# Attention values: transposed probabilities split into high and low halves, one key-value head at a time

## The chip, the cores and the metric

One NeuronCore of a Trainium2 chip runs the whole program. The metric is the device time of one execution in microseconds (us); the kernel before has a median of 1749.84 us over 3 runs (1747.56 to 1750.02).

## The reference

Two layers of a hybrid bidirectional backbone over 512 latent tokens and 256 context tokens, all in fp32. Layer 0 mixes with gated linear attention (GLA) beside grouped-query attention, layer 1 with mLSTM beside retention; every layer has an MLP. Only the attention of layer 0 is touched:

```python
def softmax_attend(q, k, v):
    s = jnp.einsum('bkgqd,bksd->bkgqs', q, k).astype(jnp.float32) * (q.shape[-1] ** -0.5)
    p = jax.nn.softmax(s, axis=-1).astype(v.dtype)
    return jnp.einsum('bkgqs,bksd->bkgqd', p, v)
...
    k_all = jnp.concatenate([k_c, k_l], axis=2)
    v_all = jnp.concatenate([v_c, v_l], axis=2)
    att_l = merge(blocked_attend(group_q(q_l), k_all, v_all).reshape(q_l.shape))
...
    att_c = merge(softmax_attend(group_q(q_c), k_c, v_c).reshape(q_c.shape))
```

There are 8 query heads of 64 in groups of g = 4 on 2 key-value heads (kv). Latent queries see all 768 keys, context queries the 256 context keys.

## The kernel before

The 768 tokens are 6 tiles t of 128; t = 0, 1 are context and see nk = 2 key tiles kt, t = 2 to 5 see nk = 6, so there are 28 pairs (t, kt). Products that want fp32 accuracy are mostly made of F32R operands: a tensor is split into a high half (a cast to F32R on ACT, L197) and a low half (a subtraction on DVE, L198), and `mm3` (L488, L489, L490) multiplies high by high, high by low and low by high, three matmuls into one accumulator. The attention is one function (L1051) with two generators:

- `scores_kv` (step S): for each t, kv and g, matmuls of 512 and 256 columns (L1093) into a PSUM tile of tag A (2 buffers), the row's maximum on DVE (L1095), and exp with its row sum on ACT (L1096) into P.
- `values` (step V), one step per key tile: for kv 0 and kv 1, four PE transposes of P (L1107) into a PSUM tile of tag B (2 buffers), copied to SBUF (tag PT, 4 buffers) by ACT for kv 0 (L1110) and by DVE for kv 1 (L1112). After the yield come two plain fp32 matmuls (L1116) of 64 stationary columns, kv 0 into the upper and kv 1 into the lower 64 partitions of one PSUM tile `po` (tag O, 1 buffer). After the last kt: reciprocal of the row sums (L1118), its transpose (L1120), copy (L1122), four matmuls with `sel` that spread it over the partitions (L1125), copy to R (L1127), and the product `po` times R on DVE (L1129). Then `finish` splits the tile into high and low (L1144, by L197 and L198): it is half of the input of the output projection.

The string PLAN["att"] writes out the order: S, V, Q (a query tile from DRAM), f (`fill`: one tile of a projection with its `mm3` matmuls, or nothing once those are used up), M (`gating`: one of four products of the GLA output, transposed at L1244 and split). The program's scheduler may still exchange neighbouring instructions when it builds, after which each engine runs its own list in order.

Three things tie the end of the attention to what follows. `sel` lies in a buffer of the tag wh, in which the high halves of weights lie too. The weights of the output projection are loaded per k = 0 to 7 (`w_out_unit`, DMAs at L540 and L541 on SP's queue for k of 4 and more) into raw buffers (tag raw, 3 of them) and split by L197 and L198; the high half of k = 4 takes the buffer of `sel`, and the raw buffer that k = 4 frees is the one into which k = 7 is loaded. And the projection's first matmuls (its k below 4 don't need the attention) stand on PE's list among and behind the last steps of the attention.

The values v (and the keys, `ak`) come out of a projection at the start, evacuated by `ev0`: one ACT copy per token tile for v (L1182).

## Time and profile before

| | |
|---|---|
| median of 3 runs | 1749.84 us (1747.56 to 1750.02) |
| profiled execution | 1746.07 us, of which the span on the core is 1744.4 us |
| mean granted TensorE clock | 0.981 |
| PE busy | 1660.3 us (95% of the span), 9795 matmuls |
| DVE busy | 1131.3 us (65%) |
| ACT busy | 791.5 us (45%) |
| POOL busy | 264.3 us (15%) |
| chain that ended last, by engine | PE 77%, DVE 9%, DMA 6%, ACT 4%, issue 3% |
| the attention's steps | from about 275 to 436 us of the span |

PE is the engine to look at over the whole program, but a share of a span is a mean over stages. The attention is a tenth of the span, and it has stretches with `fill` matmuls from other work on PE and stretches without; so the views below are taken by stretch: 275 to 367 us (steps f among the others), 367 to 417 us (none left), and 417 us on (the last query tile's values and the start of the output projection). The chain of waits lists, in order of time, what each piece of the way to the end waited for; the windows give busy time per engine in a stretch.

### The profile page before, as it was taken

The page shows a single profiled execution, that of the slowest core. Times are in us where ns is not written, and L with a number is a line of the kernel's source. Part 1 is how long each engine was busy: PE and PEld are TensorE (multiplying, and loading weights), DVE is VectorE, ACT ScalarE, POOL GpSimd, SP SyncE. Part 2 cuts the span into 40 slices and gives each one's busy share as a digit, 9 for nine tenths or more (in the row PEclk, how much of TensorE's full clock was granted, in tenths as well). Part 3 has the DMA queues.
Part 4 walks back from the last instruction along what each step waited for, and adds up shares of the span by engine and source line. Part 5 has one row for each costly group of instructions (what it writes and reads, how often), then busy time and mean ns, then how long its engine had stood idle before and what let it go on. Part 6 is the DMA issues. An engine that isn't in the chain of part 4 may idle for free.

```text
span 1744.4 us, 25127 instructions
## 1 busy us (share of the span) xinstructions
PE 1660.3 (95%) x9795; PEld 1316.5 (75%) x9795; DVE 1131.3 (65%) x1678; ACT 791.5 (45%) x1392; POOL 264.3 (15%) x216
## 2 busy tenths in 40 slices
PE   7998999999999999999999999978998999999998
PEld 5775555755778888888888878757887788888876
DVE  5435456465678558657668693466786676777876
ACT  5335435464345434334333454635552355445443
POOL 0000020100002211121120000164011112223210
PEclk9999999999999999999999999988996999999999
DMA  9415666231654224224123552234545533333322
GB/s 289 129 52 178 202 205 223 72 91 37 205 169 128 90 61 155 74 83 157 62 90 118 176 192 64 84 104 130 161 132 164 181 98 108 110 108 99 107 86 84
DMA packets 174746, 220.67 MB, mean 127 GB/s; under 512 B 17450, under 2 KB 112742, under 8 KB 174628
## 3 DMA queue, kind: packets, MB, share of 16 engines
q1 hardware_dynamic: 169444, 201.24, 36.7%
q0 software_dynamic: 5184, 17.83, 3.0%
q8 instruction: 77, 1.26, 0.3%
q14 instruction: 41, 0.34, 0.1%
HBM read 193.74 MB, written 25.30 MB: 126 GB/s over the span
## 4 chain that ended last, share of the span: by engine, by line
PE 77%; DVE 9%; DMA 6%; ACT 4%; issue 3%; SPq 1%; POOL 0%; DVEq 0%; ACTq 0%; POOLq 0%
PE x L488 21%; PE x L489 21%; PE x L490 21%; DMA x<-in_ada_w_dram 2%; PE x L1116 2%; PE x L260 2%; DVE x L198 2%; PE x L1107 1%; PE x L1093 1%; DMA x<-x 1%; ACT x L197 1%; PE x L1542 1%; PE x L957 1%; PE x L435 1%; PE x L1681 1%
## 5 line engine op out<-in xcount | busy, mean ns | idle before, releaser
L488 PE MATMUL x<-x,x 128*128 128x512 f32 (+2 forms) x2042 | 763.3, 375 | 12.1 <-ACT x L197 3.4
L489 PE MATMUL x<-x,x 128*128 128x512 f32 (+2 forms) x2050 | 762.8, 373 | 7.1 <-DVE x L198 7.1
L490 PE MATMUL x<-x,x 128*128 128x512 f32 (+2 forms) x2050 | 761.1, 372 | 0.1
L198 DVE TENSOR_TENSOR x<-x,x 128x1024 fp32r<-128x1024 f32 (+4 forms) x373 | 395.5, 1079 | 216.5 <-ACT x L197 211.4
L197 ACT CAST x<-x 128x1024 fp32r<-128x1024 f32 (+4 forms) x373 | 332.7, 911 | 388.4 <-PE x L489 181.3
L488 PEld LDWEIGHTS x<-x,x 128*128 128x128 f32 x2042 | 387.4, 190 | 91.1 <-ACT x L197 9.0
L489 PEld LDWEIGHTS x<-x,x 128*128 128x128 f32 x2050 | 389.1, 190 | 75.7 <-DVE x L198 11.7
L490 PEld LDWEIGHTS x<-x,x 128*128 128x128 f32 x2050 | 388.9, 190 | 70.6 <-issue 6.3
L638 POOL TENSOR_TENSOR x<-x,x 128x1024 f32<-128x1024 f32 x56 | 145.5, 2599 | 546.3 <-DMA x<-in_mlp_w_dram 250.2
L744 DVE TENSOR_TENSOR x<-x,x 128x512 f32<-128x512 f32 x225 | 143.9, 680 | 12.3 <-PE x L490 11.2
L689 ACT ACTIVATE x<-x 128x512 f32<-128x512 f32 (+4 forms) x96 | 44.3, 477 | 91.2 <-PE x L490 91.2
L312 DVE SCALAR_TENSOR_TENSOR x<-x,x,x 128x512 f32<-128x512 f32 x56 | 53.1, 948 | 20.8 <-DMA x<-in_ada_w_dram 19.9
L260 PE MATMUL x<-x,x 128*32 128x512 f32 x192 | 45.6, 604 | 7.5 <-DMA x<-in_ada_w_dram 7.4
L690 ACT ACTIVATE x<-x 128x512 f32<-128x512 f32 (+4 forms) x96 | 48.0, 516 | 2.1
L1095 DVE TENSOR_REDUCE x<-x 128x1 f32<-128x768 f32 (+1 forms) x48 | 36.6, 775 | 18.9 <-PE x L1093 18.7
L1116 PE MATMUL x<-x,x 128*64 128x512 f32 x112 | 44.2, 618 | 1.0 <-ACT x L1110 0.7
L1096 ACT ACTIVATE x<-x,x 128x768 f32<-128x768 f32 (+1 forms) x48 | 36.3, 757 | 12.5 <-DVE x L1095 12.3
L1107 PEld LDWEIGHTS x<-x,x 128*128 128x128 f32 x224 | 24.5, 141 | 22.9 <-issue 21.1
L675 DVE TENSOR_TENSOR x<-x 128x768 f32<-128x768 f32 (+1 forms) x28 | 38.4, 1371 | 0.0
L1093 PE MATMUL x<-x,x 128*128 128x256 f32 (+1 forms) x160 | 36.7, 347 | 1.3 <-ACT x L1096 1.3
L799 DVE TENSOR_REDUCE x<-x 128x8 f32<-128x512 f32 (+1 forms) x19 | 14.3, 753 | 35.5 <-ACT x L797 35.4
L797 ACT ACTIVATE x<-x 128x512 f32<-128x512 f32 (+1 forms) x19 | 12.8, 673 | 47.6 <-PE x L957 25.8
(316 smaller groups left out, 1517.8 us busy)
## 6 DMA issues: line engine op xcount, KB each, us to landing
x<-in_mlp_w_dram SPq DMA_DIRECT2D x128, 512.0 KB
x<-in_ada_w_dram SPq DMA_DIRECT2D x96, 512.0 KB
x<-x SPq DMA_DIRECT2D x42, 512.0 KB
x<-x SPq DMA_DIRECT2D x50, 256.0 KB
x<-in_cd_w_in_dram SPq DMA_DIRECT2D x24, 512.0 KB
x<-x POOLq DMA_DIRECT2D x36, 256.0 KB, 3.1
x<-in_ab_w_in_dram SPq DMA_DIRECT2D x16, 512.0 KB
x<-x SPq DMA_DIRECT2D x20, 384.0 KB
```

What stands on the lines that cost most here:

```text
L197: self.nc.scalar.copy(hi, src)
L198: self.nc.vector.tensor_tensor(out=lo, in0=src, in1=hi.bitcast(F32), op=ALU.subtract)
L260: nc.tensor.matmul(ps[32 * g:32 * g + 32, :n], self.sT[:, k, :], rs[g], start=k == 0, stop=k == 7)
L312: nc.vector.scalar_tensor_tensor(out=acc[x], in0=w, scalar=c, in1=acc[x], op0=ALU.mult, op1=ALU.add)
L488: mm(out, st[0], mv[0], start=start, stop=False, skip_group_check=partial)
L489: mm(out, st[0], mv[1], start=False, stop=False, skip_group_check=partial)
L490: mm(out, st[1], mv[0], start=False, stop=stop, skip_group_check=partial)
L638: sub = lambda out, x, y: nc.gpsimd.tensor_tensor(out=out, in0=x, in1=y, op=ALU.subtract)
L690: nc.scalar.activation(out=hh[:, f, c0:c1], in_=h[:, c0:c1], func=AF.Square)
L744: nc.vector.tensor_tensor(out=dst, in0=dst, in1=acc[j], op=ALU.add)
L1093: mm(pS[:, s0:s1], qs[:, h * 128:(h + 1) * 128], kst[kv][i][:, s0:s1], start=i == 0, stop=i == 1)
L1116: mm(po[64 * kv:64 * kv + 64, :], av[:, kt * 128 + kv * 64:kt * 128 + kv * 64 + 64], PT[kv], start=kt == 0, stop=kt == nk - 1)
```

## The change

- `values` takes kv in its outer loop and kt in its inner one. One step is one pair (kv, kt): four transposes (L1106), the split of their PSUM tile into high (ACT, L197) and low (DVE, L198), and after the yield two F32R matmuls (L1111), of the high and of the low half, with 128 stationary columns: v high and v low side by side.
- v is split as it is projected (`ev0`): per token tile two casts and two subtractions of 128x64 take the place of one copy; for kv 1 the halves change sides.
- `po` then holds the product with v high in one half of its partitions and that with v low in the other. After the last kt of a kv, ACT copies one half to SBUF (`sums`, L1114) and DVE adds the other (L1115). `po` has one buffer as before, so it must be emptied before the next kv's first L1111.
- The product with R is made on GpSimd (L1128), from `sums`. `sums` is the other half of the buffer that holds `sel`.
- PLAN["att"] has two V for each one before, 62 steps in place of 34.
- `ak` moves into a buffer that was already there, and `lr` shares one with X; this makes room for the larger `av`.

```diff
-            po = self.po()
-            for kt in range(nk):
-                PT = []
-                for kv in range(2):
+            for kv in range(2):
+                po = self.po()
+                for kt in range(nk):
                     pt = self.pb()
                     for g in range(4):
                         nc.tensor.transpose(pt[:, g * 128:(g + 1) * 128], P[kv][:, g, kt * 128:(kt + 1) * 128], self.C["ident"])
-                    o = self.T(at, [128, 512], F32, tag="PT", bufs=4)
-                    if kv == 0:
-                        nc.scalar.copy(o, pt)
-                    else:
-                        nc.vector.tensor_copy(o, pt)
-                    PT.append(o)
-                yield
-                for kv in range(2):
-                    mm(po[64 * kv:64 * kv + 64, :], av[:, kt * 128 + kv * 64:kt * 128 + kv * 64 + 64], PT[kv], start=kt == 0, stop=kt == nk - 1)
+                    hi, lo = [self.T(at, [128, 512], F32R, tag="PT", bufs=4) for _ in range(2)]
+                    self.split(hi, lo, pt)
+                    yield
+                    for x in (hi, lo):
+                        mm(po, av[:, kt, kv], x, start=kt == 0 and x is hi, stop=kt == nk - 1 and x is lo)
+
+                r, q = (slice(64 * x, 64 * x + 64) for x in (kv, 1 - kv))
+                nc.scalar.copy(sums[r], po[q])
+                nc.vector.tensor_tensor(out=sums[r], in0=sums[r], in1=po[r], op=ALU.add)
...
-            nc.vector.tensor_tensor(out=o, in0=po, in1=R, op=ALU.mult)
+            nc.gpsimd.tensor_tensor(out=o, in0=sums, in1=R, op=ALU.mult)
...
-        sel = self.T(self.w1, [128, 1024], F32R, tag="wh").bitcast(F32)[:8, :512]
+        sel = self.T(self.w1, [128, 1024], F32R, tag="wh").bitcast(F32)
+        sel, sums = sel[:8, :512], sel[:, 512:]
...
-                    nc.scalar.copy(av[:, t * 128:(t + 1) * 128], ps[:, 128:256])
+                    for kv in range(2):
+                        v = ps[:, 128 + kv * 64:192 + kv * 64]
+                        hi, lo = (av[:, t, kv, x * 64:x * 64 + 64] for x in (kv, 1 - kv))
+                        self.split(hi, lo, v)
...
-    "att": "QQSSSSQSSSfSVSfSSSVSfSSSVfQSSSVSSVSSSVfQfVSSVVSfVSVQSSVSSVfVSVSSVSVSSVSVSVMSVSMVVSSVSSSVVSVMVVVVVVVM",
+    "att": "QQSSSSQSSSfSVVSfSSSVVSfSSSVfQSSSVVSSVVSSSVfQfVVSSVVVVSfVVSVVQSSVVSSVfVVSVVSSVVSVVSSVVSVVSVMSVVSMVVVVSSVVSSSVVVVSVMVVVVVVVVVVVVVM",
```

How this moves instructions shows best at three places. The first is PE's list in the middle stretch, where no step f is left: scores (L1093), transposes and value matmuls alternate. x_3501 is `po` before, x_3593 is `po` now, and the tile at the head of an L1116 or L1111's sources is a transposed tile in SBUF. Before:

```order
L1116 MATMUL x_3501<-x_3564,x_655 64x512
L1116 MATMUL x_3501<-x_3571,x_655 64x512
L1107 MATMUL x_3583<-x_73,x_3270 128x128 x4
L1107 MATMUL x_3590<-x_73,x_3402 128x128 x4
L1093 MATMUL x_3598<-x_1073,x_3220 128x512
L1093 MATMUL x_3598<-x_1073,x_3220 128x256
L1093 MATMUL x_3598<-x_1073,x_3220 128x512
L1093 MATMUL x_3598<-x_1073,x_3220 128x256
L1116 MATMUL x_3501<-x_3588,x_655 64x512
```

Now:

```order
L1111 MATMUL x_3593<-x_3599,x_654 128x512
L1111 MATMUL x_3593<-x_3600,x_654 128x512
L1106 MATMUL x_3625<-x_73,x_3327 128x128 x4
L1111 MATMUL x_3593<-x_3610,x_654 128x512
L1093 MATMUL x_3653<-x_1091,x_3271 128x512
L1093 MATMUL x_3653<-x_1091,x_3271 128x256
L1093 MATMUL x_3653<-x_1091,x_3271 128x512
L1111 MATMUL x_3593<-x_3611,x_654 128x512
L1111 MATMUL x_3593<-x_3630,x_654 128x512
```

The pair of matmuls of one key tile, which stood behind eight transposes, has become two pairs, each of a high and a low half from one set of four transposes, and all for one kv; the second of a pair (from x_3611) stands behind another three score matmuls.

The second place is PE's list at the end of the attention. L488 to L490 are `mm3` matmuls of the output projection, x_4088 before and x_4303 now its first accumulators; L1120 and L1119 are the transpose of the reciprocals, L1125 and L1124 the matmuls with `sel`. Before:

```order
L1107 MATMUL x_3977<-x_73,x_3692 128x128 x4
L1107 MATMUL x_3984<-x_73,x_3801 128x128 x4
L488 MATMUL x_4088<-x_4031,x_3181 128x512
L1116 MATMUL x_3896<-x_3982,x_655 64x512
L1116 MATMUL x_3896<-x_3989,x_655 64x512
L1120 MATMUL x_3994<-x_73,x_2704 8x128
L489 MATMUL x_4088<-x_4032,x_3181 128x512
L490 MATMUL x_4088<-x_4031,x_3182 128x512
L1125 MATMUL x_3998<-x_3996,x_2696 128x128 x4
L488 MATMUL x_4088<-x_4037,x_3181 128x512
L489 MATMUL x_4088<-x_4038,x_3181 128x512
L490 MATMUL x_4088<-x_4037,x_3182 128x512
```

Now:

```order
L1111 MATMUL x_4139<-x_4179,x_654 128x512
L1106 MATMUL x_4195<-x_73,x_3961 128x128
L1111 MATMUL x_4139<-x_4189,x_654 128x512
L1106 MATMUL x_4195<-x_73,x_3961 128x128 x3
L490 MATMUL x_4360<-x_4258,x_3233 128x512
L1111 MATMUL x_4139<-x_4190,x_654 128x512
L1119 MATMUL x_4209<-x_73,x_2721 8x128
L1111 MATMUL x_4139<-x_4200,x_654 128x512
L1124 MATMUL x_4213<-x_4211,x_2713 128x128 x3
L1111 MATMUL x_4139<-x_4201,x_654 128x512
L1124 MATMUL x_4213<-x_4211,x_2713 128x128
L488 MATMUL x_4303<-x_4265,x_3230 128x512
```

Before, 4 `mm3` matmuls stood among the last query tile's key tiles, and 36 between its last L1116 and the first that needs k = 7; now 24 and 18. The transpose of the reciprocals and most matmuls with `sel` now stand ahead of the last L1111.

The third place is ACT's list there; x_4050 before and x_4265 now is the high half of the weights of k = 4, x_4084 and x_4299 that of k = 7, and the cast of 128x4x128 is `finish`. Before:

```order
L1122 COPY x_3996<-x_3994 8x128
L1127 COPY x_4003<-x_3998 128x512
L197 CAST x_4050<-x_4047 128x1024
L197 CAST x_3179<-x_4003 128x4x128
L197 CAST x_4070<-x_4067 128x1024
L197 CAST x_4077<-x_4074 128x1024
L197 CAST x_4084<-x_4081 128x1024
```

Now:

```order
L1121 COPY x_4211<-x_4209 8x128
L1114 COPY x_2713<-x_4139 64x512
L1126 COPY x_4218<-x_4213 128x512
L197 CAST x_3230<-x_4218 128x4x128
L197 CAST x_4265<-x_4262 128x1024
L197 CAST x_4285<-x_4282 128x1024
L197 CAST x_4292<-x_4289 128x1024
L197 CAST x_4299<-x_4296 128x1024
```

The copy out of `po` (L1114) has come in, and `finish`, whose source is now what GpSimd's product leaves, stands ahead of the cast of k = 4 in place of behind it. On SP's list a broadcast (L341) now stands ahead of the load of k = 7, and behind it before; behind the attention every list is the same in both.

## Rows read from the trace of the kernel before

**Rows 1.** Windows by stretch: length in us, then busy us (instructions) of PE, PEld, DVE, ACT, POOL.

```profile
275.00:340.00 65.00, 63.07 (x316) 44.40 (x314) 40.32 (x75) 37.36 (x90) 6.36 (x8) 1.00 0.39 135
340.00:367.30 27.30, 27.27 (x129) 17.87 (x128) 13.42 (x20) 15.80 (x29) 3.16 (x3) 1.00 0.12 42
367.30:417.30 50.00, 49.59 (x255) 28.76 (x253) 35.82 (x46) 29.61 (x59) 1.26 (x1) 1.00 0.32 94
417.30:436.30 19.00, 18.48 (x89) 9.74 (x89) 6.43 (x9) 5.66 (x11) 0.00 (x0) 1.00 0.00 1
```

**Rows 2.** Groups of instructions from 272 to 440 us, shapes kept apart.

```profile
L1116 PE MATMUL x<-x,x 128*64 128x512 f32 x112 | 44.2, 618 | 1.0 <-ACT x L1110 0.7
L1107 PE MATMUL x<-x,x 128*128 128x128 f32 x224 | 32.8, 280 | 0.0
L1095 DVE TENSOR_REDUCE x<-x 128x1 f32<-128x768 f32 x32 | 30.2, 953 | 5.8 <-PE x L1093 5.7
L1096 ACT ACTIVATE x<-x,x 128x768 f32<-128x768 f32 x32 | 28.8, 899 | 7.7 <-DVE x L1095 7.7
...
L1112 DVE COPY x<-x 128x512 f32<-128x512 f32 x28 | 19.3, 689 | 19.3 <-PE x L1107 19.0
L1110 ACT COPY x<-x 128x512 f32<-128x512 f32 x28 | 16.3, 583 | 26.7 <-PE x L1107 26.7
...
L1218 POOL TENSOR_TENSOR x<-x,x 128x512 f32<-128x512 f32 x6 | 7.7, 1283 | 59.4 <-DVE x L222 34.7 <-issue 24.7
```

**Rows 3.** Chain of waits in the middle stretch: start us, us, what.

```profile
367.49 0.23 PE x L490
367.71 0.87 PE x L1107 x8
...
369.29 1.00 PE x L1116 x2
...
383.53 1.02 PE x L1107 x8
...
402.72 1.01 PE x L1116 x4
...
416.55 0.59 PE x L1107 x4
```

**Rows 4.** The same chain near the first value matmuls.

```profile
290.20 0.48 ACT x L1110
...
290.72 1.07 PE x L1116 x2
```

**Rows 5.** The same chain at the end of the attention.

```profile
422.97 0.32 issue
...
432.31 1.56 PE x L1116 x4
...
436.19 1.06 ACT x L197
...
437.28 1.24 DVE x L198
...
438.53 0.47 SPq L540
...
439.05 4.35 DMA x<-in_w_out_dram
...
443.47 1.05 ACT x L197
```

**Rows 6.** TensorE's timeline, the first matmuls that need the weights of k = 7.

```profile
444.57 0.73 PE L488 MATMUL x<-x,x 128*128 128x512 f32 x2 [0.35 <-ACT x L197]
```

**Rows 7.** One line's instructions, L1182: duration ns min/median/max, first and last start us.

```profile
L1182 ACT COPY x<-x x6: 266/272/275, 73.0 to 93.0; 128x128 f32<-128x128 f32 x6
```

**Rows 8.** The page's busy tenths in 40 slices.

```profile
DVE  5435456465678558657668693466786676777876
ACT  5335435464345434334333454635552355445443
```

More of the change, by code (lines that the diff above doesn't have):

```diff
@@ L837, in gla @@
         nc.scalar.copy(lrT, pt[:, :768])
-        X, XC = self.T(ga, [128, 708]), self.T(ga, [128, 256])
+        X, XC = self.T(ga, [128, 708], tag="X", bufs=1), self.T(ga, [128, 256])
         nc.gpsimd.memset(X, 0.0)
@@ L999, in att_tables, with att_keys @@
         return gb, tabs
-    def att_keys(self, ak, gb, tab):
+    def att_keys(self, scr, gb, tab):
         nc = self.nc
         kst = self.big(self.r2, F32R)
-        scr = self.T(self.r2, [128, 3072], F32, tag="big", bufs=4)
-        kt1 = scr[:, 0:768]
+        kt1, ak = scr[:, 0:768], scr[:, 2304:]
         akv = ak.rearrange("p (x c) -> p x c", c=64)
@@ L1164, in layer0 @@
         with self.pool("mx") as mx:
-            ak, av = self.T(mx, [128, 768]), self.T(mx, [128, 768])
+            av = self.T(mx, [128, NT, 2, 128], F32R)
             gb, tabs = self.att_tables(mx)
             gqk = self.big(self.r2)
+            scr = self.T(self.r2, [128, 3072], F32, tag="big", bufs=4)
+            ak = scr[:, 2304:]
             def ev1(t, ps):
@@ L1177, in layer0 @@
                 self.C0 = self.load_consts(ga, _L0_CONST)
-                lr = self.T(ga, [128, 6, 32])
+                lr = self.T(ga, [128, 708], tag="X", bufs=1)[:, :192].rearrange("p (t n) -> p t n", t=6)
                 def ev0(t, ps):
                     nc.scalar.copy(ak[:, t * 128:(t + 1) * 128], ps[:, 0:128])
-                    nc.scalar.copy(av[:, t * 128:(t + 1) * 128], ps[:, 128:256])
+                    for kv in range(2):
+                        v = ps[:, 128 + kv * 64:192 + kv * 64]
+                        hi, lo = (av[:, t, kv, x * 64:x * 64 + 64] for x in (kv, 1 - kv))
+                        self.split(hi, lo, v)
                     nc.vector.tensor_copy(lr[:, t], ps[:, 256:288])
@@ L1188, in layer0 @@
                               lambda t, ps: nc.scalar.copy(tok4(gv, t), ps.rearrange("p (r n) -> p r n", r=4)), True)
-                kst = self.att_keys(ak, gb, tabs[1])
+                kst = self.att_keys(scr, gb, tabs[1])
                 late = []
```

## The prediction, before the change was run

> **What bounds the kernel now.** I read the windows first, since the change touches a tenth of the program. In all four stretches PE is busy nearly throughout: 63.1 of 65.0 us, 27.3 of 27.3, 49.6 of 50.0, 18.5 of 19.0, at a granted clock of 1.00 [rows 1]. DVE has 35.8 and ACT 29.6 of the 50.0 us in the middle stretch [rows 1]: loaded, but not the bound. So time comes from PE first, and the question is how much of it DVE and ACT let through.
>
> Then the groups by shape: the value matmuls L1116 hold PE for 44.2 us, the transposes L1107 for 32.8 [rows 2]. The chain shows what they cost: two records of one fp32 matmul alone take 1.00 us; the four records of a pair of heads, when both are ready, take 1.01, because the two use different columns of the array; when the second copy is late they take up to 1.56 [rows 3, 5]. A pair always overlapped would give 28 x 1.01 = 28.3 us, the row has 44.2, so most pairs run mostly one after the other. An F32R matmul of 512 columns takes 0.23 us in the chain [rows 3]. After fp32 or scores there is a small entry cost: eight transposes take 0.87 us behind F32R work and 1.02 behind L1116 [rows 3].
>
> Last the chain at the end. The last L1116 piece begins at 432.31 and lasts 1.56 us; after it the chain leaves PE: the cast and subtraction of the weights k = 4 (they wait for the buffer of `sel`), SP's issue, a transfer of 4.35 us, the cast of k = 7 [rows 5], whose first matmul is at 444.57 [rows 6]. From 433.87 to that is 10.7 us, in which PE has 36 `mm3` matmuls (8.3 us at 0.23) and L1125 (some 1.1) to run. So this end is tied by two things at once: PE's work, and the chain through the weights.
>
> **The change, part by part.**
>
> *Value matmuls.* 56 fp32 matmuls (112 records, 44.2 us) become 112 in F32R: 112 x 0.23 = 25.8. Freed: 18.4. There are 56 short groups of transposes instead of 28 pairs; 28 more entries at 0 to 0.15 us (1.02 - 0.87) are 0 to 4.2 us. I take 1.4, nearer the lower end, since they stand between F32R work now. **PE work freed: 17.0 us.** By stretch, at 0.61 per pair (17.0 / 28): some 5.6 to 275-367 us, 7.3 to the middle, 3.6 to the last tile.
>
> *Evacuation.* Before, ACT copies kv 0 (583 ns) and DVE kv 1 (689 ns), side by side [rows 2]. Now each of the 56 transposed tiles goes through ACT and then DVE. That is 28 more passes on ACT (16.3 us) and 28 more on DVE (19.3 us), plus 12 ACT copies (at most 7.0) and 12 adds (at most 8.3) out of `po`, less six products on DVE (4.1). And the path from transposes to matmul grows by a DVE pass: about 0.6 + 0.7 and some 0.4 of handovers (0.32 from PE to ACT, 0.03 from ACT to DVE [rows 5]) instead of 0.6 or 0.7, with only two PSUM buffers and four PT tiles to run ahead.
>
> *Middle stretch* (367.71 to 416.55 in the chain, 48.8 us [rows 3], 12 pairs, no filler). PE's own work falls to some 41.5. DVE: 35.8 + 12 more passes and 4 adds less 2 products (14 x 0.69 = 9.7) is 45.5. ACT: 29.6 + 16 passes (9.4) is 39. I followed the three lists against each other with these durations: 46.3 us. So **-2.5**; bounds -6 (PE's work and two entry waits alone) and +2 (DVE's 45.5 with some 5 us of waits at either end).
>
> *First stretches* (92 us, 10 pairs). PE frees 5.6, but the first value matmuls already wait for an ACT copy that stands behind other work (chain: ACT to 290.68, then L1116 at 290.72 [rows 4]); there a DVE pass and its queue come on top, 1 to 2 us twice. **-2.0**; bounds -5.6 and +1.5.
>
> *Last tile* (416.55 to 433.87, 17.3 us). Here 20 more `mm3` matmuls (4.6 us) now stand among the key tiles, so PE's work is: transposes 48 x 0.11 and entries 5.9, L1111 24 x 0.23 = 5.5, `mm3` 5.5, six more transposes 0.7, in all 17.6. The waits for cast and subtraction that the fillers don't cover add some 2.6: 20.2. **+2.9**; bounds 0 and +4.
>
> *End.* The buffer of `sel` now comes free only after `po` is emptied, `sums` added and GpSimd's product made; and `finish`, which waits for that product, stands ahead of the cast of k = 4 on ACT and holds it and the three casts behind it. From the last L1111: copy 0.6, add 0.7, product 1.28 (as L1218 [rows 2]), `finish` 0.6, then cast 1.06, subtraction 1.24, issue 0.47, transfer 4.35, cast 1.05 [rows 5], and some 0.6 for handovers (0.32 to ACT, 0.03 to 0.07 for the others [rows 5]): 11.9 against 10.7. **+1.2**; bounds +0.5 and +2.7 (the broadcast now ahead of this load on SP's queue costs up to three issues of 0.47). PE has only 18 `mm3` matmuls and a rest of L1124 for these 11.9 us, some 4.4, so it idles for 7: that is where the freed time comes out.
>
> *v split.* Twelve casts and twelve subtractions of 128x64 for six copies of 0.27 us [rows 7]: at 0.27 each, a longest side of DVE + 3.2 us. At 73 to 93 us DVE and ACT are 3 to 5 tenths busy (slices 2 and 3 [rows 8]) and PE's projection runs on other accumulators: 0, bounds 0 and +0.5. The single `po` makes a kv's first L1111 wait for copy and add (1.3 us) twelve times; four transposes and scores stand ahead of it on PE each time, so this is inside the walks above.
>
> **Sum:** -2.5 - 2.0 + 2.9 + 1.2 = -0.4 us, so 1745.7 for the profiled execution of 1746.07. That one stands 3.8 below the median of 1749.84; against the median it is 1749.4.
>
> The Trainium skill, "TensorEngine Tiling (Array Packing)", section "Theoretical Speedup", speaks against giving up the narrow tiles: a matrix side of 64 or less lets two tiles run in parallel, for an estimate of 2 times. By that rule alone the old pairs would cost 28.3 us and the change would free 2.5 instead of 18.4; the 44.2 us of the row says that the rule is met in few pairs here, and the measurement decides.
>
> **Rivals.**
>
> *A. PE stays the bound and the evacuation keeps up.* Then the middle gives -6, the first stretches -5.6, the last tile +1 (17.6 and entry gaps), the end +1.2: -9.4, **1740**. For it: PE at 97 to 100% in every stretch [rows 1], DVE with 14 us idle in the middle one. Against: DVE's 45.5 there lies above PE's 41.5.
>
> *B. Slower: the evacuation becomes the bound.* The place is DVE's list in the middle stretch: every L198 waits for its L197, and the maxima of the scores (953 ns, 32 of them [rows 2]) stand in the same list, so each wait delays the next scores and with them exp and the next transposes. It decides once DVE's sum with its waits passes the 48.8 us of today: 45.5 and 24 waits of 0.25 (below the 0.32 between a transpose and its ACT copy [rows 5]) are 51.5, +2.7. The first stretches then give +1.5, the last tile and the end as above: +8.3, **1758**. For it: two engines in series with two PSUM buffers leave little to run ahead. Against: before their copies DVE and ACT now sit idle for 19.0 and 26.7 us, waiting for the transposes [rows 2], and that is room.
>
> The Trainium skill, the same page, section "PSUM Bottleneck", warns of this case: faster tiles do nothing for the emptying of PSUM, which may become the bottleneck, and both ScalarE and VectorE should share it. Here both already do, but in series after the change; no row of before shows that.
>
> *C. The change doesn't do what it says:* the F32R form with 128 stationary columns takes as long as fp32. 112 x 1.00 would add 68 us. The L490 piece of 0.23 is the same type and width, so next to nothing.
>
> **How the numbers follow.** About 0.2% (3.5 us) is what a measurement of this kernel can tell from no change. My forecast, no change that can be told, gets 0.38; A 0.34, B 0.27, C 0.01. The forecast's own range is 1746 to 1753. With cases of both signs holding most of the chance, the range of 8 in 10 takes in A's 1740 and B's 1758, and a microsecond beyond each for the unknown entries and for SP's order: 1739 to 1759. The two outermost sums of all bounds, -11 and +11, lie at its edges. Faster 0.35 (A and a little of the forecast's edge), same 0.38, slower 0.27.
>
> **What would show it.** L1111 112 times at 0.23 us apart. In the middle stretch DVE above nine tenths with waits of L198 on L197, and a length near 46 us; near 42 is A, above 50 is B. The last tile near 20 us. PE idle for some 7 us between the last L1111 and the k = 7 matmuls, with the chain L1114, add, GpSimd's product of 1.28, `finish`, k = 4, DMA. I am wrong if the projection's start does not wait for GpSimd, if L1111 pairs stand further apart than transposes explain, or if stretches outside 275 to 446 us change by over 2 us.

## The result, and the profile after

The changed kernel takes 1760.56 us (median of 4 runs, 1758.71 to 1762.69) where the kernel before took 1748.70 (4 runs, 1745.82 to 1750.02): a ratio of 1.007 with a 95% interval of 1.0051 to 1.009. It is 12 us slower. The forecast was 1749.4 and no change that can be told; the range ended at 1759.

The profiled execution took 1759.3 us, its span 1757.5. To see where the time went I cut both traces at the same landmarks: the first score matmul, the last fill matmul, the first transpose of the last query tile, the end of the last value matmul, the first matmul that needs the weights of k = 7, and one `mm3` matmul behind it (the 276th L490). The windows between them, before the change (columns as in [rows 1]; behind POOL stand the granted clock, the DMA engines' busy share and the GB/s that they moved):

```profile
274.98:367.10 92.12, 90.17 (x443) 62.10 (x442) 53.54 (x94) 52.96 (x119) 9.54 (x11) 1.00 0.31 108
367.10:416.48 49.38, 48.97 (x249) 28.29 (x247) 35.66 (x46) 29.16 (x57) 1.26 (x1) 1.00 0.33 96
416.48:433.86 17.38, 16.86 (x83) 8.53 (x82) 6.79 (x10) 5.47 (x9) 0.00 (x0) 1.00 0.00 1
433.86:444.57 10.71, 10.36 (x48) 7.72 (x48) 4.99 (x7) 5.36 (x7) 1.12 (x2) 1.00 0.41 130
444.57:460.02 15.45, 14.92 (x65) 12.04 (x66) 6.45 (x12) 4.77 (x12) 0.25 (x1) 1.00 0.76 250
```

and after:

```profile
277.76:370.31 92.55, 87.95 (x442) 68.17 (x442) 62.44 (x106) 60.59 (x134) 12.60 (x14) 0.98 0.31 106
370.31:419.42 49.11, 43.14 (x247) 32.80 (x245) 43.72 (x58) 37.03 (x73) 3.33 (x3) 1.00 0.33 94
419.42:440.48 21.06, 20.57 (x113) 15.34 (x111) 11.65 (x17) 10.37 (x19) 1.29 (x1) 1.00 0.00 1
440.48:459.25 18.77, 7.14 (x21) 4.81 (x20) 4.98 (x7) 5.67 (x7) 2.38 (x3) 0.74 0.67 171
459.25:475.95 16.70, 16.66 (x65) 13.16 (x66) 6.45 (x12) 4.76 (x12) 0.25 (x1) 0.88 0.42 122
```

| stretch | before | after | change | forecast |
|---|---|---|---|---|
| first score matmul to last fill | 92.1 | 92.6 | +0.4 | -2.0 |
| middle | 49.4 | 49.1 | -0.3 | -2.5 |
| last tile | 17.4 | 21.1 | +3.7 | +2.9 |
| end: last value matmul to k = 7 | 10.7 | 18.8 | +8.1 | +1.2 |
| behind it, to the same `mm3` | 15.4 | 16.7 | +1.3 | 0 |
| sum | 185.0 | 198.2 | +13.2 | -0.4 |

Where the first score matmul falls is no reading of the change: it lies between 273.5 and 283.8 us in the 14 profiles of these experiments, of kernels with either attention, and at 277.8 in this one against 275.0 before. So the lengths of stretches are compared here, not their starts. (The time ahead of the first landmark is 2.8 us longer in this profile than before, the time behind the last one 2.8 us shorter; within that spread neither can be put down to the change.)

Two things are to be seen. In the first two stretches PE was freed, by 2.2 and 5.8 busy us, and they are as long as they were: PE's idle time grew from 2.0 to 4.6 us and from 0.4 to 6.0. And at the end PE has 7.1 busy us of 18.8. What PE waited for from the first score matmul to the last value matmul is led by one row in both kernels (us in total, times, longest us), before and after:

```profile
PE x L1093 <- ACT x L1096: 1.3, 2, 1.1
```

```profile
PE x L1093 <- ACT x L1096: 4.4, 8, 0.8
```

These are scores that wait for the exp on ACT, which leaves their PSUM tile free. After the change 2.6 us of waits of the value matmuls for cast and subtraction come with it (0.7 for their copies before), and 1.9 of `fill`'s matmuls for ACT's casts (none of 0.2 us or more before). The groups of the changed kernel that answer to [rows 2], from 272 to 446 us:

```profile
L1111 PE MATMUL x<-x,x 128*128 128x512 f32 x112 | 44.1, 442 | 3.1 <-DVE x L198 1.3 <-ACT x L197 1.3
L198 DVE TENSOR_TENSOR x<-x,x 128x512 fp32r<-128x512 f32 x62 | 41.8, 686 | 14.2 <-ACT x L197 13.5
L197 ACT CAST x<-x 128x512 fp32r<-128x512 f32 x62 | 35.7, 588 | 22.3 <-PE x L1106 17.4 <-POOL x L1128 2.9 <-PE x L1111 1.4
L1106 PE MATMUL x<-x,x 128*128 128x128 f32 x224 | 33.3, 272 | 0.0
...
L1128 POOL TENSOR_TENSOR x<-x,x 128x512 f32<-128x512 f32 x6 | 7.8, 1296 | 86.8 <-DVE x L1115 61.0 <-ACT x L1126 25.8
```

L198 and L197 have 62 of these shapes, 56 of them for transposed tiles; DVE stood 13.5 us waiting for ACT's casts ahead of L198, where its copies waited 19.0 us for the transposes before [rows 2]. The busy time of L1111 (44.1 us, as much as L1116 had) is no price of a matmul: a matmul's bar is 442 ns long here, and in the chain below two that stand together take 0.46 us (428.49), as forecast. But one that stands among transposes takes 0.37 (434.42). Counted from each start to the next instruction's start on PE, less idle time, the 31 that stand right behind another L1111 take 0.24 on the mean, those right behind a transpose 0.35, and all 112 together 32.7 us (0.29 each). The 112 records of L1116 took 41.7 by the same count, and the transposes as long as before. So 9.0 us were freed, not the 17.0 of the forecast.

The chain at the end, in order of time (start us, us, what), answers to [rows 5]:

```profile
428.49 0.46 PE x L1111 x2
...
434.42 0.37 PE x L1111
...
440.06 0.44 PE x L1111
...
440.52 0.59 ACT x L1114
...
441.13 0.70 DVE x L1115
...
442.02 1.24 POOL x L1128
...
443.81 1.05 ACT x L197
...
444.88 1.24 DVE x L198
...
446.13 0.47 SPq L540
...
446.65 11.43 DMA x<-in_w_out_dram
...
458.16 1.05 ACT x L197
...
459.25 0.79 PE x L488
```

and SP's queue at the same time:

```profile
444.70 0.33 SPq L341 DMA_DIRECT2D x<-x  x1
446.13 0.47 SPq L540 DMA_DIRECT2D x<-in_w_out_dram  x1
446.65 0.67 SPq L541 DMA_DIRECT2D x<-in_w_out_dram  x1
```

Before, SP issued the load at 438.53 [rows 5] and the broadcasts behind it:

```profile
440.07 1.29 SPq L341 DMA_DIRECT2D x<-x  x3
```

The links from the last L1111 to SP's issue at 446.13 take 5.7 us, as the forecast had them (5.5 and the handovers). The transfer takes 11.43 us where it took 4.35 [rows 5]. In SP's queue the broadcast L341 was issued 1.4 us ahead of it. A second order turned round as well: GpSimd issues two loads of inputs of 512 KB each (L576), before 1.2 us behind the load's issue, and now 0.9 us ahead of it. Before and after:

```profile
439.78 1.12 POOL L576 DMA_DIRECT2D x<-in_ctx_dram  x2 [63.06 <-DVE x L1297]
```

```profile
445.21 1.12 POOL L576 DMA_DIRECT2D x<-in_ctx_dram  x2 [1.96 <-DVE x L1302]
```

### The profile page after: what moved, and what is told of

Its sections match the earlier page's. It is cut to its first block, busy times and chain, and to the rows that moved or that the text cites. A ratio compares the mean times of both kernels' runs of the same rounds, so it can differ in the third digit from the quotient of the medians.

```text
span 1757.5 us, 25288 instructions
## 1 busy us (share of the span) xinstructions
PE 1654.1 (94%) x9795; PEld 1329.6 (76%) x9795; DVE 1154.2 (66%) x1724; ACT 813.0 (46%) x1438; POOL 272.4 (16%) x222
## 4 chain that ended last, share of the span: by engine, by line
PE 56%; DVE 8%; DMA 5%; ACT 4%; issue 3%; POOL 1%; SPq 1%; DVEq 0%; ACTq 0%; POOLq 0%
PE x L488 17%; PE x L489 17%; PE x L490 17%; DMA x<-x 2%; DVE x L198 2%; ACT x L197 1%; DMA x<-in_mlp_w_dram 1%; DMA x<-in_w_out_dram 1%; PE x L1111 1%; PE x L435 1%; PE x L1547 1%; PE x L1686 1%; PE x L1685 0%; DMA x<-in_cd_w_in_dram 0%; DVE x L744 0%
## 5 line engine op out<-in xcount | busy, mean ns | idle before, releaser
L488 PE MATMUL x<-x,x 128*128 128x512 f32 (+2 forms) x2042 | 765.9, 376 | 25.6 <-ACT x L197 16.8
L490 PE MATMUL x<-x,x 128*128 128x512 f32 (+2 forms) x2050 | 762.4, 373 | 0.1
L198 DVE TENSOR_TENSOR x<-x,x 128x1024 fp32r<-128x1024 f32 (+5 forms) x441 | 436.7, 1009 | 244.0 <-ACT x L197 238.3
L197 ACT CAST x<-x 128x1024 fp32r<-128x1024 f32 (+5 forms) x441 | 367.1, 851 | 422.4 <-PE x L489 180.3
L488 PEld LDWEIGHTS x<-x,x 128*128 128x128 f32 x2042 | 388.6, 191 | 106.1 <-ACT x L197 22.8
L490 PEld LDWEIGHTS x<-x,x 128*128 128x128 f32 x2050 | 389.8, 190 | 71.1 <-issue 6.3
L744 DVE TENSOR_TENSOR x<-x,x 128x512 f32<-128x512 f32 x225 | 143.8, 680 | 12.1 <-PE x L490 11.2
L689 ACT ACTIVATE x<-x 128x512 f32<-128x512 f32 (+4 forms) x96 | 44.3, 476 | 91.4 <-PE x L490 91.4
L1095 DVE TENSOR_REDUCE x<-x 128x1 f32<-128x768 f32 (+1 forms) x48 | 36.5, 774 | 17.7 <-PE x L1093 17.6
L1111 PE MATMUL x<-x,x 128*128 128x512 f32 x112 | 44.1, 442 | 3.1 <-DVE x L198 1.3
L1093 PE MATMUL x<-x,x 128*128 128x256 f32 (+1 forms) x160 | 38.4, 351 | 4.6 <-ACT x L1096 4.4
L1093 PEld LDWEIGHTS x<-x,x 128*128 128x128 f32 x160 | 26.6, 195 | 12.2 <-ACT x L1096 9.5
L427 ACT ACTIVATE x<-x 128x1024 f32<-128x1024 f32 x16 | 17.0, 1060 | 36.7 <-DVE x L445 28.2
```

Source lines behind the costliest of these rows:

```text
L197: self.nc.scalar.copy(hi, src)
L198: self.nc.vector.tensor_tensor(out=lo, in0=src, in1=hi.bitcast(F32), op=ALU.subtract)
L488: mm(out, st[0], mv[0], start=start, stop=False, skip_group_check=partial)
L490: mm(out, st[1], mv[0], start=False, stop=stop, skip_group_check=partial)
L744: nc.vector.tensor_tensor(out=dst, in0=dst, in1=acc[j], op=ALU.add)
L1093: mm(pS[:, s0:s1], qs[:, h * 128:(h + 1) * 128], kst[kv][i][:, s0:s1], start=i == 0, stop=i == 1)
```

## The experiments

Each median stands against runs of the kernel before made beside it on the same chip (medians 1744.2 to 1746.9), and runs are compared by how far each lies from its own: the changed kernel 11.9 us above. Stretches are named as in the table, in the same order: first, middle, last tile, end, behind. Their sum, set against the 185.0 us of the kernel before, agrees with the difference of the medians within 4.5 us in the changed kernel and in the twelve runs where all five were read; where the two differ, the stretches are the finer reading, though they come from one profile.

### The end: the transfer, the buffer, the product

**The broadcasts behind the load.** One element of the raw weights of k = 7 is copied into each broadcast's tile before its DMA.

```diff
+        if after is not None:
+            self.nc.vector.tensor_copy(t[:1, :1], after[:1, :1])
         j = 0 if stream == "lat" else 1
         self.nc.sync.dma_start(out=t, in_=md[j:j + 1, o:o + 1024].to_broadcast([128, 1024]))
...
```

> The changed kernel, with one thing added: the three broadcasts of modulation rows that follow the attention may start only when the weights of k = 7 have landed (one element of these is copied into each broadcast's tile first), so that none stands ahead of that load in SP's queue. Theory Q (the load of k = 7 is slow, 11.4 us against 4.4 before, because a 512 KB broadcast is issued 1.4 us ahead of it): the load takes 4 to 6 us again, PE's gap from the last value matmul to the first matmul of k = 7 falls from 18.7 to about 12, and the time by 6 to 8 us, to about 1753. Rival (everything in flight shares the bandwidth and order does not matter, or the broadcasts, now late, hold up the first normalisation as long): the time stays within 2 us of 1760.

Measured: 1754.90 against 1746.88, ratio 1.0049 (1.0027 to 1.007): 8.0 us above, 3.8 less than the changed kernel. The end fell from 18.8 to 14.1 us, the transfer from 11.43:

```profile
443.60 6.73 DMA x<-in_w_out_dram
```

Theory Q holds for 4.7 of the 8.1 us in these two profiles. That size is loose: the transfer took 7.9 to 11.4 us in the six profiles with a broadcast issued ahead of it. A transfer that is still 2.4 us longer than before remains. Here GpSimd's two loads were still issued 0.9 us ahead of the load, as in those six; in the nine profiles in which the transfer took 4.0 to 4.4 us, both they and the broadcasts were issued behind it. So GpSimd's loads may well be the rest; no run moved them alone.

**The sums out of the buffer of `sel`.**

```diff
-        sel, sums = sel[:8, :512], sel[:, 512:]
+        sel = sel[:8, :512]
...
+            sums = P[0].rearrange("p g n -> p (g n)")[:, :512]
```

> The changed kernel with the sums out of the buffer of sel (they go into P's own tile of kv 0, which is no longer needed by then), so the high half of k = 4 waits only for the matmuls with sel, as before the change. On SP's list the load of k = 7 then stands ahead of the broadcasts again. Theory E (the loss is the end: the chain through copy, add, GpSimd's product and finish to k = 4, and behind it the late load of k = 7): the load is issued some 3 us sooner after the last value matmul and takes 4 to 6 us; 8 to 11 us are won, to about 1751, which is the kernel before within 3 us. Rival B (the loss is the evacuation of the transposes in the attention, DVE's list being the bound): at most 3 us are won, 1757 to 1760.

Measured: 1751.66, ratio 1.0027 (1.0006 to 1.0048): 4.8 us above, 7.1 less than the changed kernel. The stretches are 91.9, 49.5, 21.1, 10.0 and 15.3: the attention is untouched, the end is back. Its chain has this transfer, which SP issued at 442.13, the broadcasts 1.5 us later and GpSimd's loads 1.2 us later:

```profile
442.65 4.26 DMA x<-in_w_out_dram
```

Theory E holds. Against the kernel before the last tile has 3.7 us more, and the end 0.7 less.

**The product on DVE**, in the changed kernel and with the sums elsewhere:

```diff
-            nc.gpsimd.tensor_tensor(out=o, in0=sums, in1=R, op=ALU.mult)
+            nc.vector.tensor_tensor(out=o, in0=sums, in1=R, op=ALU.mult)
```

> The changed kernel with the last product on DVE (0.69 us) in place of GpSimd (1.28); SP's list is unchanged, so the broadcast still stands ahead of the load of k = 7. Theory E with Q: the chain at the end is 0.6 us shorter and the load still takes 11 us: 0 to -1.5 us, 1759 to 1761. Rival (GpSimd is what holds the end): -4 us or more.

> Sums out of the buffer of sel as in the run before, and the product on DVE as well. With the sums elsewhere the product is on the way only of finish for the last tile, so theory E expects within 1.5 us of that run, about 1750. If DVE is the bound in the attention (rival B), six more products of 0.69 us there cost 2 to 4 us against it.

Measured: 1757.69, ratio 1.0051 (1.0021 to 1.0081), and 1750.40, ratio 1.0013 (0.9993 to 1.0032). The first is 10.8 us above, 1.1 less than the changed kernel, as forecast. Its profiled execution took 1745.91, 12 us less than its median, so that profile is a poor witness: there the last tile is 18.4 in place of 21.1 and the transfer 8.02 in place of 11.43. The list of the last tile changed with it (the gating's casts and products stand earlier, and its transposes with them), so the 2.7 us of the last tile are the product and this order together; I did not separate them. The second is 1.3 below its partner, as forecast. It cannot be told from the kernel before.

**The end alone, in the kernel before.** `po` is copied to the other half of the buffer of `sel`, and GpSimd multiplies the copy; all else is the kernel before.

```diff
...
-            nc.vector.tensor_tensor(out=o, in0=po, in1=R, op=ALU.mult)
+            nc.scalar.copy(sums, po)
+            nc.gpsimd.tensor_tensor(out=o, in0=sums, in1=R, op=ALU.mult)
```

> The kernel before with only the change's end: po is copied by ACT to the other half of the buffer of sel, and GpSimd multiplies that copy with R; value matmuls, transposes and v stay as before. On SP's list one broadcast then stands ahead of the load of k = 7, as in the changed kernel. Theory E (the end carries most of the loss): from the last value matmul to the first matmul of k = 7 grows from 10.7 to 16 to 19 us, the load taking 8 to 11 us, the next stretch by 1.2 at the lower clock, and the first two stretches stay within 1 us of 92.1 and 49.4: 7 to 11 us slower, 1753 to 1758 where the kernel before has 1746.7. Rival (the end hurts only together with the F32R value matmuls, because the filler was moved up): at most 3 us slower.

Measured: 1755.91 against 1745.78, ratio 1.0056 (1.004 to 1.0073). The five windows:

```profile
275.24:368.06 92.82, 90.69 (x442) 62.15 (x441) 51.79 (x90) 54.50 (x122) 13.37 (x14) 1.00 0.31 106
368.06:417.41 49.35, 47.91 (x249) 28.23 (x248) 34.66 (x45) 29.98 (x59) 2.56 (x2) 1.00 0.32 96
417.41:435.12 17.71, 17.47 (x83) 8.55 (x82) 6.11 (x9) 5.48 (x9) 1.27 (x1) 1.00 0.00 1
435.12:452.78 17.66, 10.60 (x48) 7.64 (x47) 4.29 (x6) 5.84 (x8) 2.41 (x3) 0.94 0.60 190
452.78:469.80 17.02, 16.98 (x65) 13.39 (x66) 6.45 (x12) 4.77 (x12) 0.24 (x1) 0.86 0.39 112
```

and the transfer in its chain:

```profile
442.85 8.76 DMA x<-in_w_out_dram
```

10 us slower with none of the new value matmuls: the end grows by 7.0, the stretch behind it by 1.6, and the attention stays within 0.7 us in each stretch. This is most of the loss of the changed kernel, made in the other kernel. The broadcast was issued 1.4 us ahead of the load here too, and GpSimd's loads 0.9.

### The attention: where TensorE's freed time went

**No subtraction.** Both value matmuls read the high half; the low half is left out.

```diff
-                    self.split(hi, lo, pt)
+                    nc.scalar.copy(hi, pt)
                     yield
-                    for x in (hi, lo):
-                        mm(po, av[:, kt, kv], x, start=kt == 0 and x is hi, stop=kt == nk - 1 and x is lo)
+                    for i in range(2):
+                        mm(po, av[:, kt, kv], hi, start=kt == 0 and i == 0, stop=kt == nk - 1 and i == 1)
```

> The changed kernel without the subtraction behind each transpose: both value matmuls read the high half (the low half of P is left out, and the high one counted twice). PE and ACT keep every instruction, the buffers stay two passes deep, DVE loses 56 x 0.69 us, 24 of them in the middle stretch. Theory B (the ACT-then-DVE evacuation bounds the attention): from the first score matmul to the last fill matmul falls from 92.6 to 87 to 89, the middle stretch from 49.1 to 42 to 45, the last tile from 21.1 to 18 to 19; 10 to 14 us in all. Rival P (TensorE's own entries, order and switches between forms eat the freed time): these stretches stay within 1 us.

Measured: 1751.70, ratio 1.003 (1.0011 to 1.0049): 5.1 us above, 6.8 less than the changed kernel. The first three windows:

```profile
280.56:370.96 90.40, 85.75 (x442) 67.11 (x442) 50.00 (x86) 60.57 (x135) 13.21 (x14) 0.99 0.31 106
370.96:415.67 44.71, 41.22 (x249) 33.22 (x247) 30.19 (x37) 36.98 (x73) 2.57 (x2) 1.00 0.38 106
415.67:431.62 15.95, 15.07 (x86) 11.02 (x85) 2.65 (x4) 9.09 (x17) 1.28 (x1) 1.00 0.00 1
```

The first stretch fell by 2.2 (less than forecast) and the middle by 4.4: 6.6 us for the subtraction, on lists of PE that are as long as before (442 and 249 instructions against 442 and 247). The last tile's 5.1 are mostly something else: PE has 86 instructions there in place of 113, among them 7 `mm3` matmuls in place of 24, and the others stand at the end, where PE idled (43 instructions in place of 21). Of the 6.6 us only 2.5 are idle time of PE that is gone, all in the middle; 4.1 are busy time (in the first stretch some of it may be the clock: its first 30 us were granted 0.98 in place of 0.92). With one operand to wait for, 65 of the 112 value matmuls stand right behind another (31 with the subtraction), and counted from start to start all 112 take 28.9 us in place of 32.7. So the subtraction costs TensorE in two ways, in waits and in matmuls that no longer stand together.

**One pass, ACT and DVE in turn.** The same, with the cast by key tile on one engine or the other.

```diff
-                    nc.scalar.copy(hi, pt)
+                    (nc.vector.tensor_copy if kt % 2 else nc.scalar.copy)(hi, pt)
```

> As the run without the subtraction, and the one pass that is left goes to ACT and DVE in turn, by key tile, as one engine per transposed tile had it before the change (the low half of P is left out as there). Theory B in the form that a pass's latency and DVE's sum decide: the middle stretch near 42 to 45, within 1.5 us of the run without the subtraction. If ACT's casts alone had become the bound there, it is over 2 us shorter than that run. Rival P: 48 to 49 in both.

Measured: 1747.20, ratio 1.0 (0.998 to 1.002); stretches 91.5, 44.2, 17.1, 16.5, 16.8. The middle is within 0.5 us of the run before it: ACT's casts alone do not bound it.

**One emptying of `po` per query tile.** The heads of both kv are added up in one `po`; their separation is left out.

```diff
-            for kv in range(2):
-                po = self.po()
+            po = self.po()
+            for kv in range(2):
...
-                        mm(po, av[:, kt, kv], x, start=kt == 0 and x is hi, stop=kt == nk - 1 and x is lo)
+                        mm(po, av[:, kt, kv], x, start=kv == 0 and kt == 0 and x is hi, stop=kv == 1 and kt == nk - 1 and x is lo)
+                if kv == 0:
+                    continue
...
-                nc.scalar.copy(sums[r], po[q])
+                nc.scalar.copy(sums, po)
```

> The changed kernel with one accumulation over both kv per query tile (the heads of the two kv are added up, which leaves out the separation of the heads), so po is emptied 6 times and not 12: six copies of 0.59 us on ACT and six adds of 0.69 on DVE fewer, and no wait of kv 1's first matmul for the emptying of kv 0's. Theory H (the single po and its emptying hold the first stretches): these fall from 92.5 by 2 to 4 us, the middle from 49.1 by 1 to 2. Rival (it is the subtraction alone, whose removal gave 2.2, 4.4 and 5.1 us): each stretch within 1 us.

Measured: 1753.48 against 1745.78, ratio 1.0049 (1.0024 to 1.0074). First 90.2 (-2.4, as theory H had it), middle 48.4 (-0.7, less than it asked), last tile 18.5 (-2.6). PE's idle time falls by 1.9 us in the first stretch and as much in the middle. The last tile has 12 instructions of PE fewer, so some of its 2.6 is order. So the single `po` and its twelve emptyings are a second, smaller cost, in the first stretch above all; the forecast had held them covered. The wait for `po` and the six copies and adds that went with it are not told apart here.

**Two tries to use the freed time.** Steps f moved later in the order string (with some V earlier and the M later), and, in another run, the gating's products moved to GpSimd; both on top of the kernel with sums elsewhere and the product on DVE.

```diff
-    "att": "...fQfVVSSVVVVSfVVSVVQSSVVSSVfVVSVVSSVVSVVSSVVSVVSVMSVVSMVVVVSSVVSSSVVVVSVMVVVVVVVVVVVVVM",
+    "att": "...fQfVVSSVVVVSVVSVVfQSSVVSSVVVSVVSSfVVSVVSSVVSVVSVSVVSVVVVMSSVVSMSSVVVVSVMVVVVVVVVVVVVVM",
```

> Sums out of the buffer of sel and the product on DVE as in an earlier run, and the order string rewritten: the last two steps f stand some 6 and 12 steps later, steps V earlier against them, and the four M later by a few steps, so that projection matmuls stand where DVE bounds the attention. Theory B: the 92 us of the first stretches fall by about the 11 us of two steps f and the middle grows by less, 4 to 8; 3 to 7 us in all, 1743 to 1747 where that run had 1750. Rival P: the sum of the stretches stays within 1.5 us.

Measured: 1749.31, ratio 1.0005 (0.998 to 1.0029). First, middle and last tile are 98.6, 42.6 and 20.6, in sum 161.7 against 159.2 in the run it was made from: the time moved with the steps. A miss.

```diff
-                    nc.vector.tensor_tensor(out=sg[:, i], in0=sg[:, i], in1=on[:, i], op=ALU.mult)
+                    nc.gpsimd.tensor_tensor(out=sg[:, i], in0=sg[:, i], in1=on[:, i], op=ALU.mult)
```

> Sums out of the buffer of sel and product on DVE as before, and the four products of the gating (0.95 us each on DVE, three of them in the middle stretch) on GpSimd, which takes some 1.9 us for each by its 1.28 per 512. If DVE's sum bounds the middle stretch (theory B), that stretch falls from 48.6 by 2 to 3 us, and the time to 1747 to 1749, level with the kernel before. Rival (GpSimd's products delay the gating or slow DVE down): 48 to 51.

Measured: 1747.16 against 1745.78, ratio 1.0003 (0.9986 to 1.002). DVE's middle window fell from 45.5 to 42.3 busy us and the stretch went from 48.6 to 49.3. The middle's window:

```profile
367.64:416.95 49.31, 43.59 (x251) 33.29 (x249) 42.28 (x57) 37.52 (x74) 9.61 (x5) 1.00 0.32 93
```

So DVE's sum alone does not set the middle's length: with 7 us of DVE idle it is no shorter, and DVE's wait for ACT's casts ahead of L198 rose from 0.7 to 5.1 us. That speaks for the serial path (transposes, cast, subtraction, matmul) through two PSUM buffers. It is argued, not shown: the rival put on record, that GpSimd's products hold up the gating (1.8 us and more each, 0.94 on DVE), asked for the same length, and the order of the lists changed too.

**The narrow pairs.** The kernel before, with both halves of a key tile in one SBUF tile; the scheduler was to set more pairs side by side by it.

```diff
+                PT = self.T(at, [128, 1024], F32, tag="PT", bufs=2).rearrange("p (v n) -> p v n", v=2)
+                PT = [PT[:, 0], PT[:, 1]]
...
-                    o = self.T(at, [128, 512], F32, tag="PT", bufs=4)
+                    o = PT[kv]
...
```

> The kernel before with both transposed halves of a key tile in one SBUF tile, nothing else: the scheduler then sets 22 of 28 pairs of narrow fp32 matmuls next to each other on TensorE's list, where it set fewer before. Theory T (a pair of 64-column matmuls runs in the time of one when both stand together and are ready, 1.01 us): the value matmuls fall from 44.2 busy us to 34 to 40 and the attention by 3 to 8 us, 1739 to 1744 against 1747. Rival (the second copy is late as often, so PE waits where it worked before): within 2 us of the kernel before.

Measured: 1747.10 against 1746.64, ratio 1.0001 (0.9979 to 1.0022); L1116 has 44.3 busy us. But in the traces the pairs that ran side by side are as many as before: 19 groups of two matmuls and 18 single ones in both. The edit did not bring about what it was made for, so this run does not say what side by side would give. It shows how well stretches repeat: their sum is 184.3, and 185.0 before. In the kernel before, 7 of the 19 groups took 1.01 to 1.05 us, the others 1.15 to 1.55, and a single matmul some 1.00.

### Both repairs, and what they point to

**End and subtraction together:** the edits of the sums elsewhere, of the product on DVE and of the run without the subtraction.

> Both repairs at once: sums out of the buffer of sel with the product on DVE, and no subtraction behind the transposes (the low half of P is left out, the high one counted twice). Theory (two losses in series, the end's transfer and DVE's subtraction, cover the time that TensorE was freed): they add up. The earlier runs gave 10 us for the end and product, and 9 for the subtraction; together 1739 to 1744, 3 to 8 below the kernel before, with the middle stretch at 44 to 45, the end near 10 and no lower clock behind it. Rival (they are one loss seen twice, or TensorE's freed work was never on the path): 1747 to 1751.

Measured: 1732.64 against 1746.59, ratio 0.9918 (0.9896 to 0.9939). 14 us below the kernel before (10.2 by the stretches), more than forecast, with the stretches 89.5, 44.1, 16.0, 9.8 and 15.5. The two losses are separate, and in the stretches they nearly add up: from 198.2 us the end's repair with the product on DVE takes 14.1, the missing subtraction 11.2, both together 23.4. The medians gain more than that (8.3, 6.8 and 25.8), which no stretch explains. TensorE's freed time shows once both covers are off.

**Only the high half of P.** With the subtraction gone the second matmul only repeats the first. On the kernel with sums elsewhere and the product on DVE, without low half and second matmul, and then with the cast on both engines in turn:

```diff
-                    hi, lo = [self.T(at, [128, 512], F32R, tag="PT", bufs=4) for _ in range(2)]
-                    self.split(hi, lo, pt)
+                    hi = self.T(at, [128, 512], F32R, tag="PT", bufs=4)
+                    nc.scalar.copy(hi, pt)
                     yield
-                    for x in (hi, lo):
-                        mm(po, av[:, kt, kv], x, start=kt == 0 and x is hi, stop=kt == nk - 1 and x is lo)
+                    mm(po, av[:, kt, kv], hi, start=kt == 0, stop=kt == nk - 1)
```

```diff
-                    nc.scalar.copy(hi, pt)
+                    (nc.vector.tensor_copy if kt % 2 else nc.scalar.copy)(hi, pt)
```

> Sums out of the buffer of sel, product on DVE, and only the high half of P: no subtraction and one value matmul per transposed tile in place of two (the low half of P, its rounding rest, is left out; v keeps both halves). PT's four buffers then hold four passes. PE loses 56 x 0.23 = 12.9 us against the run that read the high half twice, ACT and DVE nothing. If TensorE bounds the attention again once DVE's subtraction is gone (theory B, second half), 7 to 12 us of that appear: 1721 to 1727 where that run had 1732.6. Rival (ACT's casts and the scores' maxima and exp bound it by then): 0 to 4 us, 1729 to 1733.

> The same with the cast of the transposed tile on ACT and DVE in turn, by key tile. If ACT's list bounds the stretches by then, this is 2 to 6 us below the run with all casts on ACT; if TensorE does, within 2 us of it.

Measured: 1724.07, ratio 0.9876 (0.9856 to 0.9895), and 1722.16, ratio 0.9869 (0.9844 to 0.9894), against 1744.23. The first three windows with all casts on ACT:

```profile
277.52:365.23 87.71, 82.18 (x423) 64.54 (x422) 51.82 (x89) 60.23 (x135) 9.53 (x11) 0.98 0.35 117
365.23:404.72 39.49, 36.42 (x222) 28.79 (x221) 29.55 (x36) 35.31 (x71) 1.27 (x1) 1.00 0.41 117
404.72:418.41 13.69, 13.19 (x80) 9.81 (x79) 4.34 (x7) 10.02 (x20) 0.00 (x0) 1.00 0.00 0
```

The sum of the five stretches falls from 174.8 to 166.3 us, 8.5 for the 12.9 of TensorE's that were expected (11.2 by its busy time in the first three): TensorE bounds most of it again. The second has 166.2, so ACT's casts do not. One thing goes with it that was not separated: the four buffers of transposed tiles now hold four passes in place of two. This is the fastest form found, 20 to 22 us below the kernel before. It rounds the probabilities to F32R, which neither kernel does; whoever uses it has to want that.

## Why the prediction was wrong

**The end (+1.2 forecast, +8.1 and +1.3 behind it measured) is the step that failed most.** The forecast's chain was right link by link up to SP's issue: 5.7 us from the last value matmul, 4.7 before. Two terms behind it were wrong. "The broadcast now ahead of this load on SP's queue costs up to three issues of 0.47" counted the time to issue a DMA, not the 512 KB that it then moves ahead of the load: the transfer took 11.43 us in place of 4.35, and with the broadcasts held back, 6.73. GpSimd's loads, now ahead of it too, were not in the forecast at all. The Trainium skill, "DMA: Bandwidth & Descriptors", section "Queues, rings and completion order", says that each DMA engine consumes the descriptors of one issuing queue in ring order; these runs agree (4.0 to 4.4 us where the load was issued first, 7.9 to 11.4 where a broadcast was). The 6.73, with nothing ahead of it on SP's queue, is not explained by it. The second was left out altogether: after the two idle stretches of 4.0 and 7.6 us PE's granted clock is lower. In TensorE's timeline of the changed kernel the first matmuls of k = 7 start 0.43 us apart, later ones 0.23:

```profile
444.90 1.22 PE L488 MATMUL x<-x,x 128*128 128x512 f32 x2 [4.01 <-ACT x L197]
...
459.25 1.22 PE L488 MATMUL x<-x,x 128*128 128x512 f32 x2 [7.58 <-ACT x L197]
...
461.96 0.63 PE L489 MATMUL x<-x,x 128*128 128x512 f32 x1
462.39 0.63 PE L490 MATMUL x<-x,x 128*128 128x512 f32 x1
...
464.15 0.40 PE L490 MATMUL x<-x,x 128*128 128x512 f32 x1
464.38 0.39 PE L488 MATMUL x<-x,x 128*128 128x512 f32 x1
```

The granted clock of that window is 0.88 and of the one before it 0.74 (the windows above), between the levels of 1.2 and 2.4 GHz; where the gap is short (sums elsewhere) the stretch behind has 1.00 and is 15.3 us long. That is the +1.3.

**Middle and first stretch (-2.5, -2.0 forecast; -0.3, +0.4 measured).** The step that failed here is the freed time of the value matmuls, 17.0 us in the forecast and 9.0 by the starts in the traces. Its old price, 44.2, was a sum of bars (41.7 from start to start), and its new one, 0.23, holds for a matmul right behind another of its kind, as 31 of the 112 stand (0.29 on the mean of all); the 1.4 us allowed for entries were too few. (The share of ten pairs at 0.61 is also 6.1, not the 5.6 that the forecast gave the first stretch.) By the windows PE's busy time fell by 2.2 and 5.8 us where the forecast had 5.6 and 7.3. The waits were nearly right: PE's idle time grew by 2.6 and 5.6 us where the forecast had 3.6 and 4.8. Part of the first stretch's shortfall is the clock: in its first 30 us PE has 27.2 busy us at a granted clock of 0.92, where it had 29.5 at 1.00. From 296 to 302 us the clock is 0.72, behind two waits of PE of 0.7 and 1.1 us, and four score matmuls of 256 columns take 1.05 us there (from 296.73) where they took 0.48 (from 291.33). How much each part weighs was not separated.

**Last tile (+2.9 forecast, +3.7 measured)** was near in size, in part by luck. The forecast had 17.6 us of PE's own work and 2.6 of waits; measured are 20.6 busy us and 0.5 idle. **The v split at nothing** cannot be told from the profiles: the stretches before the scores vary by more than its 3 us from run to run.

**The rivals.** B came nearest in time (1758) and named the evacuation, but it was near by luck: it too had the end at +1.2, and its middle was to grow by 2.7 and did not. PE's new waits in the first two stretches (8.2 us) are as large as what its busy time lost there (8.0), no more. The Trainium skill's warning that the emptying of PSUM may become the bottleneck ("TensorEngine Tiling (Array Packing)", section "PSUM Bottleneck") is borne out in kind by the run without the subtraction, -6.6 us in its first two stretches. A is out: TensorE did not stay the bound. C is out: two that stand together take 0.46 us. The doubling from narrow tiles that the same page of the Trainium skill states, by which the change would have freed 2.5 us, was reached by 7 of the 19 pairs that ran side by side; what more of them would give was not tested.

## What to carry to other kernels

When a matmul gets cheaper by an operand that must first be split, the split is a serial path of two engines: take one link out in an experiment before counting TensorE's gain. Price a matmul from start to start, with what will stand next to it on the list, and not by its bar or by its time in a row of its own kind. A buffer borrowed from a later stage (here half of a weight's tile) ties that stage to the last reader; look at what waits for the buffer, and what gets into the DMA queue ahead of it meanwhile. Price a DMA that is overtaken by the other's bytes, not by its issue, and look at the loads that other engines issue too.

## What the runs showed of the hardware

A DVE subtraction of 128x512 with both sources in SBUF took 1.59 us in the changed kernel while GpSimd's product ran, and 0.68 to 0.69 in its five other occurrences:

```profile
L1041 DVE TENSOR_TENSOR x<-x x6: 679/688/1591, 166.9 to 306.4; 128x512 f32<-128x512 f32 x6
```

```profile
306.39 1.59 DVE L1041 TENSOR_TENSOR x<-x 128x512 f32<-128x512 f32 x1 [0.38 <-ACT x L1040]
```

```profile
306.16 1.27 POOL L1128 TENSOR_TENSOR x<-x,x 128x512 f32<-128x512 f32 x1 [19.11 <-DVE x L1115]
```

DVE's bar begins 0.23 us into GpSimd's and ends 0.55 after it, which fits work that was done only behind it. The Trainium skill, "SBUF — State Buffer", section "SBUF: two separate sides", states this as a lock: a DVE operation with two SBUF inputs and a GpSimd operation that reads SBUF share a pair of ports, and the later one is held for the whole of the other. This occurrence agrees, and so does one more: at 377.03 us a subtraction of 128x1024 (L198, weights in SBUF) took 1.99 us beside another product of GpSimd (L1223, 376.65 to 377.93), where the other eleven of its kind up to 460 us took 1.21 to 1.23. The subtractions behind the transposes, which read PSUM, kept 0.68 to 0.69 us beside GpSimd's products. The product of the change was put on GpSimd to spare DVE, and here it cost DVE 0.9.
